# A decoder layer in fp32: the norms behind the output projections, in whole rows of x

## Chip, cores and metric

The kernel runs on one core of one Trainium2 chip. The metric is the device time of one execution in microseconds, the median of several runs.

## The reference

One decoder layer for 2048 tokens of 1024 channels, everything in fp32:

```python
hn = rms_norm(h, mix_pre_g)
proj = hn @ w_in                     # q, k, v and the convolution's input u
attn_out = sliding_window_attention(q, k, v, attn_sinks, rel_bias)   # window 128, 8 heads of 64
conv_out = conformer_conv(u, ...)    # GLU, causal depthwise conv of width 31, LayerNorm, silu, w_conv_pw
mixed = jnp.concatenate([attn_out, conv_out], axis=-1) @ w_out
h = h + rms_norm(mixed, mix_post_g)
hn = rms_norm(h, ffn_pre_g)
ff = (jax.nn.silu(hn @ w_gate) * (hn @ w_up)) @ w_down
h = h + rms_norm(ff, ffn_post_g)
```

`rms_norm(x, g)` is x times the reciprocal root of its mean square, times g. The change concerns the first `h = h + rms_norm(mixed, ...)` and the line behind it, where `hn` is stored without its gain.

## The kernel before

Tokens are worked on in four slices of 512 (w = 0 to 3), each of four tiles of 128 rows. Every large product is made as three fp32r matmuls, from a high and a low part of each operand: ACT copies the high part (`split_w` L123, L127), DVE or POOL subtracts it to get the low part (L129, `lo`). A "product" in the text is one bank of PSUM, 12 or 24 matmuls of 128x512. Names in the profile end in the stage: @A is the input projection (`stage_a`), @B the attention (`stage_b`), @C the convolution (`stage_taps`, `stage_tail`), @W the output projection with its norms (`stage_w` L706, `norm_w` L759), @H the transposes of `hn` into operands of the feed-forward part, @F its gate and up products, @G its down products.

The stages are generators in lanes (`Lane` L1284, `run` L1363): while one stage emits its products, each lane is given credit at a rate, and a stage in a lane emits its next piece when its credit is positive. `yield c` says how much credit a piece costs. A scheduler then orders the instructions of each engine. So W0 stands among the products of A3, W1 ahead of F0, W2 and W3 among those of G0. W_LEAD = 4.0 (L1334) is a piece of that credit, waited at a stage's start.

Tiles come from rotating pools (`BUFS` L53): a new tile of a tag waits until the tile that had its buffer is released. Of 4 KB per partition (one row tile of 1024, or a high and low pair of 512) there are x 4, p 4, mid 4, hl 8, ql 4, chl 5, wx 1; of 2 KB (one half row) gb 2, fa 4, at 2. The tag fa is also A's: ACT puts the block of V into one (L398), from which PE transposes it (L407) and DVE copies it to `vtok` (L410). L418 and a DVE difference put q into `ql`. The tag chl holds operands of W1 to W3. There are four mm banks.

Most loads and stores are issued by SP, in one order: w@A (L126) and raw (L137, L914) weights, mixT (L717), gains `rows` (L697), x (L778, L784), h_scr (L786), keeps (L921), mids and td (L1146, L1150) for G. A DMA that has to wait for its buffer or its data holds up those behind it. ACT's queue issues hn_scr (L797) and mixT (L520).

The norm of one slice goes over its four row tiles `acc[s]`:

1. ACT squares each (L765) with a sum, and `rsqrt` (L144) makes four numbers per partition from them, in 3 small operations on DVE and 12 on POOL (all on DVE for W3).
2. DVE scales `acc[s]` by r and by the gain in two operations of 512 columns (`post_scale` L700, recorded at L94 as are most DVE operations).
3. x is added: one row tile of the four as a whole row in wx, the others as halves in fa or at. For W1 to W3 DVE adds (WV); for W0 POOL adds two of the four row tiles (L779, L785).
4. SP stores the sum to h_scr, ACT squares it (L787).
5. After a second `rsqrt`, ACT scales each row tile in place (L794) and its queue stores hn_scr.

`stage_p1`, `stage_h_plain` and `stage_h_sums` read hn_scr turned, later.

## Time and profile before

| | |
|---|---|
| median of 3 runs | 2044.41 us (2039.39 to 2044.48) |
| the profiled execution | 2052.75 us |
| its span, first to last instruction | 2051.0 us |
| mean granted clock of TensorE | 0.981 |
| busy: PE, DVE, ACT, POOL | 1956.7, 1471.4, 953.2, 367.8 us |

PE is TensorE's matmuls, PEld its weight loads, DVE VectorE, ACT ScalarE, POOL GpSimd, SP the engine that issues most DMAs. A wait is written "engine tile line <- engine tile line": the first waited, for the second, followed by us in total, times and the longest. A row of a timeline has start, duration, engine, line, operation, output <- inputs, shapes, count, and in brackets the idle time before it and what ended it. A group of instructions has its count, busy us, mean ns of one, and the idle time before them with what ended it. The word "issue" in such a bracket means that the profile shows nothing that the engine waited for. The granted clock is TensorE's, as a share of full speed.

### The profile page before, as it was taken

What the parts mean: (1) busy time and instruction counts of PE and PEld (TensorE: products, weight loads), DVE (VectorE), ACT (ScalarE), POOL (GpSimd) and SP (SyncE); (2) the same over time, 40 slices, a digit from 0 to 9 for tenths busy, and PEclk for the clock granted to TensorE, in tenths of its full rate; (3) what the DMA queues carried; (4) which work ended last, traced back from release to release, by engine and by line L of the source; (5) the groups of instructions that cost most, each with busy time, mean ns of one, the idle gap of its engine ahead of it and who ended that gap; (6) DMA issues with size and microseconds to landing.
All of it is one profiled execution on the core that took longest, in us unless ns stands there. A gap on an engine that the chain in (4) does not pass through costs nothing.

```text
span 2051.0 us, 26796 instructions
## 1 busy us (share of the span) xinstructions
PE 1956.7 (95%) x8730; PEld 1556.6 (76%) x8730; DVE 1471.4 (72%) x2583; ACT 953.2 (46%) x1878; POOL 367.8 (18%) x438
## 2 busy tenths in 40 slices
PE   8999998998988899899999989999999999999997
PEld 6777776676756778678878777777878888888886
DVE  4999979967656789788748973678466665545557
ACT  5355354445736634333336454574544434345443
POOL 4012232114011300000000010035323323221003
PEclk9999999999999999999999999999999999999999
DMA  8787655458758875886467787697954443266654
GB/s 301 250 308 237 202 199 184 161 190 267 250 176 280 277 269 196 279 289 202 154 221 240 242 303 232 212 325 242 311 184 153 160 167 113 99 225 225 203 188 148
DMA packets 232028, 454.57 MB, mean 222 GB/s; under 512 B 23208, under 2 KB 48976, under 8 KB 231888
## 3 DMA queue, kind: packets, MB, share of 16 engines
q1 hardware_dynamic: 213648, 426.64, 61.9%
q10 hardware_dynamic: 18240, 26.22, 3.5%
q8 instruction: 69, 1.13, 0.2%
q14 instruction: 71, 0.58, 0.1%
HBM read 331.65 MB, written 121.12 MB: 221 GB/s over the span
## 4 chain that ended last, share of the span: by engine, by line
PE 59%; DMA 16%; DVE 15%; issue 4%; ACT 3%; POOL 2%; SPq 1%; DVEq 0%; ACTq 0%; POOLq 0%
PE mm@F L85 28%; PE mm@G L85 11%; PE mm@A L85 9%; DVE fc@C L94 5%; PE mm@W L85 4%; PE tr@B L85 3%; PE tr@W L85 2%; DVE hl@G L94 2%; DMA mixT<-fc@C 2%; DMA at@W<-mixT 1%; DMA gb@F<-keeps 1%; DVE mid@W L94 1%; DVE w@F L94 1%; DMA td<-fc@G 1%; DVE sm@G L94 1%
## 5 line engine op out<-in xcount | busy, mean ns | idle before, releaser
L94 DVE SCALAR_TENSOR_TENSOR fc@C<-glu@C,colt,fc@C 128x512 f32<-128x512 f32 x480 | 370.6, 790 | 2.6
L85 PE MATMUL mm@F<-hl@H,w@F 128*128 128x512 f32 x1056 | 258.4, 394 | 12.0 <-ACT mm@F L936 10.3
L85 PE MATMUL mm@G<-hl@G,hl@G 128*128 128x512 f32 x924 | 236.0, 395 | 9.8 <-ACT mm@G L1219 3.9
L85 PEld LDWEIGHTS mm@F<-hl@H,w@F 128*128 128x128 f32 x1056 | 199.5, 190 | 57.5 <-ACT mm@F L936 13.5
L85 PE MATMUL mm@A<-hl@A,w@A 128*128 128x512 f32 x840 | 212.5, 400 | 5.1 <-ACT w@A L127 2.4
L85 PEld LDWEIGHTS mm@G<-hl@G,hl@G 128*128 128x128 f32 x924 | 173.4, 190 | 48.4 <-DVE hl@G L94 4.6
L85 PE MATMUL mm@G<-w@G,hl@G 128*128 128x512 f32 x876 | 199.4, 389 | 0.0
L809 ACT ACTIVATE w@F<-chl@F 128x512 fp32r<-128x512 f32 x220 | 134.8, 624 | 129.6 <-PE mm@F L85 122.8
L85 PEld LDWEIGHTS mm@A<-hl@A,w@A 128*128 128x128 f32 x840 | 158.3, 191 | 43.2 <-ACT w@A L127 3.0
L85 PEld LDWEIGHTS mm@G<-w@G,hl@G 128*128 128x128 f32 x876 | 164.4, 188 | 34.2
L94 DVE TENSOR_TENSOR w@F<-chl@F,w@F 128x512 fp32r<-128x512 f32 x198 | 145.0, 734 | 38.6 <-ACT w@F L809 38.3
L85 PE MATMUL mm@F<-ql@H,w@F 128*128 128x512 f32 x528 | 131.5, 397 | 13.6 <-ACT mm@F L1043 5.6
L85 PE MATMUL mm@F<-mid@H,w@F 128*128 128x512 f32 x528 | 132.6, 397 | 0.9 <-DVE fa@F L94 0.3
L85 PE MATMUL mm@F<-p@H,w@F 128*128 128x512 f32 x528 | 130.0, 391 | 0.0
L85 PEld LDWEIGHTS mm@F<-ql@H,w@F 128*128 128x128 f32 x528 | 100.2, 191 | 37.2 <-ACT mm@F L1043 6.6
L85 PE MATMUL mm@F<-x@H,w@F 128*128 128x512 f32 x528 | 127.0, 391 | 0.8 <-ACT fa@F L958 0.8
L85 PEld LDWEIGHTS mm@F<-mid@H,w@F 128*128 128x128 f32 x528 | 100.4, 191 | 23.9 <-ACT mm@F L936 1.1
L85 PEld LDWEIGHTS mm@F<-p@H,w@F 128*128 128x128 f32 x528 | 100.0, 189 | 21.0
L85 PEld LDWEIGHTS mm@F<-x@H,w@F 128*128 128x128 f32 x528 | 98.4, 188 | 22.5 <-ACT fa@F L958 1.3
L127 ACT ACTIVATE w@A<-raw@A 128x512 fp32r<-128x512 f32 x110 | 67.5, 626 | 96.8 <-PE mm@A L85 63.6
L494 POOL TENSOR_SCALAR_AFFINE_SELECT p@B<-p@B 128x512 f32<-128x512 f32 x62 | 51.6, 843 | 278.0 <-ACT p@B L492 276.5
L94 DVE TENSOR_TENSOR w@G<-raw@G,w@G 128x512 fp32r<-128x512 f32 x73 | 52.5, 719 | 67.3 <-ACT w@G L809 66.3
(303 smaller groups left out, 3365.3 us busy)
## 6 DMA issues: line engine op xcount, KB each, us to landing
mids<-fa@F SPq DMA_DIRECT2D x154, 256.0 KB, 2.6
raw@A<-w_in SPq DMA_DIRECT2D x55, 512.0 KB, 4.6
w@A<-lo_in SPq DMA_DIRECT2D x84, 256.0 KB, 3.7
fc@G<-mids SPq DMA_DIRECT2D x77, 256.0 KB, 3.4
fa@G<-mids SPq DMA_DIRECT2D x75, 256.0 KB, 5.0
gb@F<-keeps SPq DMA_DIRECT2D x72, 256.0 KB, 4.2
w@W<-fold SPq DMA_DIRECT2D x32, 512.0 KB, 5.6
chl@F<-w_gate SPq DMA_DIRECT2D x22, 512.0 KB, 3.8
```

What stands on the lines that cost most here:

```text
L85: r = nc.tensor.matmul(*args, **kw)
L94: r = op(*args, **kw)
L127: act(w[:, 0], raw, AF.Copy)
L494: nc.gpsimd.affine_select(out=pg[:, kb].rearrange("p (i q) -> p i q", q=P), in_=pg[:, 1].rearrange("p (i q) -> p i q", q=P), compare_op=AL ...
L809: act(w[:, 0], x, AF.Copy)
```

## The change

- The gain is one whole row tile in chl (before: two halves in gb). The four row tiles of x are whole tiles in chl, asked for as soon as the first `rsqrt` has been emitted (before: halves in fa and at and a whole one in wx, each asked for at its addition).
- The scale is one operation of 1024 columns per row tile (before: two of 512), and so is the addition, always on DVE (before: POOL too for W0; WV is gone).
- The last scale of ACT writes into the x tile rather than in place, and is followed at once by its store to hn_scr; `hns`, which nothing reads, goes.
- The pieces of credit grow: squares 0.5 to 0.75, each scale with its addition 1.5 to 1.25 + 1.25, the last scales 0.1 for all to 1.25 each. W0 gets W_LEAD at its start as well, which only W1 to W3 had.

```diff
@@ -690,20 +690,7 @@
                 vtt(acc[i][:, cs], acc[i][:, cs], o, ALU.add)
             yield 0.65 * len(units)
 
-    def load_gb(row):
-        gb = []
-        for n in range(2):
-            t = f2("gb")
-            nc.sync.dma_start(t, rows[row, n * T : (n + 1) * T].partition_broadcast(P))
-            gb.append(t)
-        return gb
-
-    def post_scale(acc, gb, r):
-        for n in range(2):
-            cs = slice(n * T, (n + 1) * T)
-            stt(acc[:, cs], acc[:, cs], r, gb[n], ALU.mult, ALU.mult)
-
-    def stage_w(w, spill, atag, htags, mtag, bank_of, norm=None, ready=None):
+    def stage_w(w, atag, htags, mtag, bank_of, norm=None, ready=None):
         G = KC // len(htags)
         L = f"W{w}"
         lab[0] = L
@@ -733,8 +720,7 @@
             return ws
 
         nxt = acts(0)
-        if G == 4:
-            yield W_LEAD
+        yield W_LEAD
         for gi in range(KC // G):
             aa = nxt
             for n in range(2):
@@ -750,55 +736,50 @@
                         lab[0] = L
                         nxt = acts(gi + 1)
                     yield c
-        tail = norm_w(w, spill, acc, mtag)
+        tail = norm_w(w, acc)
         if norm:
             norm(tail)
         else:
             yield from tail
 
-    def norm_w(w, spill, acc, mtag):
+    def norm_w(w, acc):
         L = f"W{w}"
         lab[0] = L
-        gb = load_gb(0)
+
+        def whole(src):
+            t = f4("chl")
+            nc.sync.dma_start(t, src)
+            return t
+
+        gb = whole(rows[0].partition_broadcast(P))
         ssq = sm(4)
         for s in range(4):
             act(junk, acc[s], AF.Square, accum_out=ssq[:, s : s + 1])
-            yield 0.5
+            yield 0.75
             lab[0] = L
         r = rsqrt(ssq, 4, D, w < 3)
+        xs = [whole(x[w * T + s * P : w * T + (s + 1) * P]) for s in range(4)]
+        ssq2 = sm(4)
         yield 3
-        lab[0] = L
-        ssq2 = sm(4)
         for s in range(4):
             lab[0] = L
-            post_scale(acc[s], gb, r[:, s : s + 1])
+            stt(acc[s], acc[s], r[:, s : s + 1], gb, ALU.mult, ALU.mult)
+            yield 1.25
+            lab[0] = L
+            vtt(acc[s], xs[s], acc[s], ALU.add)
             r0 = w * T + s * P
-            if s == (2 if mtag == "fa" else 0):
-                xt = f4("wx")
-                nc.sync.dma_start(xt, x[r0 : r0 + P])
-                (vtt if w in WV else ptt)(acc[s], xt, acc[s], ALU.add)
-            else:
-                for n in range(2):
-                    cs = slice(n * T, (n + 1) * T)
-                    xt = f2(mtag if s == 1 or w > 1 else "fa")
-                    nc.sync.dma_start(xt, x[r0 : r0 + P, cs])
-                    (vtt if w in WV or w == 0 and s % 2 else ptt)(acc[s][:, cs], xt, acc[s][:, cs], ALU.add)
             nc.sync.dma_start(h_scr[r0 : r0 + P], acc[s])
             act(junk, acc[s], AF.Square, accum_out=ssq2[:, s : s + 1])
-            yield 1.5
+            yield 1.25
         lab[0] = L
         r2 = rsqrt(ssq2, 4, D, w < 3)
         yield 3
-        lab[0] = L
         for s in range(4):
-            act(acc[s], acc[s], AF.Copy, scale=r2[:, s : s + 1])
-            if spill:
-                r0 = w * T + s * P
-                nc.scalar.dma_start(hn_scr[r0 : r0 + P], acc[s])
-        yield 0.1
-        hns[w] = acc
-
-    hns = {}
+            lab[0] = L
+            act(xs[s], acc[s], AF.Copy, scale=r2[:, s : s + 1])
+            r0 = w * T + s * P
+            nc.scalar.dma_start(hn_scr[r0 : r0 + P], xs[s])
+            yield 1.25
 
     def load_cols(w, k, tag):
         t = f2(tag, (P, 4, P))
@@ -1344,7 +1325,6 @@
     PRES = {0: 20, 2: 16}
     Q0 = 8
     POOL_LO = (3, 6)
-    WV = [1, 2, 3]
     PRE_S0, PRE_S2 = 22, 16
     H1, H2, H3, H4 = 0, 4, 7, 11
     lb = Lane(RB, 0)
@@ -1373,7 +1353,7 @@
 
     lb.add("X", stage_x(), lambda: "x1" in started)
     lu.add("U", stage_fold(), lambda: "A2" in started)
-    lw.add("W0", stage_w(0, True, "x", ["hl"] * 4, "fa", mm), lambda: "A3" in started and "C0" in ld.done and "U" in lu.done)
+    lw.add("W0", stage_w(0, "x", ["hl"] * 4, "fa", mm), lambda: "A3" in started and "C0" in ld.done and "U" in lu.done)
     TGA = [["hl"] * 8, ["mid"] * 4 + ["chl"] * 4, ["hl"] * 8, ["mid"] * 4 + ["hl"] * 4]
     xa = {}
     warm = mm()
@@ -1426,7 +1406,7 @@
     ws, ops = (0, 1), {}
     for n, off in (("B11", 0), ("B21", 4)):
         lh.add(n + ".0", stage_h_plain(ws, ops, n, off))
-    run(stage_w(1, True, "mid", ["hl", "chl"], "at", mm, norm=lambda g: lh.add("N1", g), ready=lambda: stage_pre(ws, ops, mids[0], keeps[0], 0, Q0)))
+    run(stage_w(1, "mid", ["hl", "chl"], "at", mm, norm=lambda g: lh.add("N1", g), ready=lambda: stage_pre(ws, ops, mids[0], keeps[0], 0, Q0)))
     lc.hold = lambda: "S0" not in lh.done
     lh.until("B21.0")
     lh.add("S0", stage_h_sums(ws, ops), lambda: f"P0.{PRE_S0}" in started and "B3" in lb.done)
@@ -1438,9 +1418,9 @@
     lc.rates["T3"] = RC3
     ws, ops = (2, 3), {}
     lw.add("C2", stage_tail(2))
-    lw.add("W2", stage_w(2, True, "mid", ["ql", "chl"], "at", tr))
+    lw.add("W2", stage_w(2, "mid", ["ql", "chl"], "at", tr))
     lw.add("C3", stage_tail(3), lambda: since(lc, "T3", CS))
-    lw.add("W3", stage_w(3, True, "mid", ["ql", "chl"], "at", tr, norm=lambda g: lw.add("N3", g)))
+    lw.add("W3", stage_w(3, "mid", ["ql", "chl"], "at", tr, norm=lambda g: lw.add("N3", g)))
     lw.add("B11.2", stage_h_plain(ws, ops, "B11", 0))
     run(stage_p2((0, 1), mids[0], td))
     lw.until("N3")
```

In the new file the x and gain loads stand at line 751, the squares at 757 and 772, h_scr at 771, the last scale at 779, hn_scr at 781, W's mixT loads and splits at 704 and 706, raw for F at 895.

The scheduler decides what follows from this on each engine. Three places, before and after.

**ACT at W0's norm**. L398 is the copy of V into fa, L418 that of q, L127 a weight's high part, L787 (new: L772) the second squares, L518 and L520 the attention's. Before:

```order
L418 ACTIVATE ql@A_763_4650<-mm@A_761_4618 128x512
L127 ACTIVATE w@A_776_4739<-raw@A_774_4734 128x512
L398 ACTIVATE fa@A_754_4579<-mm@A_753_4554 128x512
L787 ACTIVATE junk,sm@W_742_4508<-x@W_572_3572 128x1024
L518 ACTIVATE at@B_737_4466<-tr@B_736_4461 128x512
L787 ACTIVATE junk,sm@W_742_4508<-x@W_573_3573 128x1024
L520 DMA mixT<-at@B_737_4466 128x4x128
L787 ACTIVATE junk,sm@W_742_4508<-x@W_574_3574 128x1024
L787 ACTIVATE junk,sm@W_742_4508<-x@W_575_3575 128x1024
```

After:

```order
L398 ACTIVATE fa@A_750_4548<-mm@A_749_4523 128x512
L127 ACTIVATE w@A_767_4685<-raw@A_765_4680 128x512
L603 ACTIVATE fc@C_616_3772<-ct@C_615_3767,lnh 128x512
L605 ACTIVATE fc@C_617_3774<-ct@C_615_3767,lnh 128x512
L518 ACTIVATE at@B_731_4439<-tr@B_730_4434 128x512
L127 ACTIVATE w@A_771_4721<-raw@A_770_4719 128x512
L520 DMA mixT<-at@B_731_4439 128x4x128
L772 ACTIVATE junk,sm@W_745_4514<-x@W_572_3572 128x1024
L706 ACTIVATE hl@W_780_4771<-at@W_779_4769 128x512
L418 ACTIVATE ql@A_756_4602<-mm@A_754_4570 128x512
L127 ACTIVATE w@A_772_4724<-raw@A_770_4719 128x512
```

The copy of V has moved ahead of all second squares, and the copy of q and the next split of w@A behind the first of them.

**DVE at the same place**, from the scales to the copy of V into vtok (L410). x@W are the accumulated rows, sm@W the reciprocal roots, fc@C the taps of the convolution. Before, where L410 comes 5 rows behind the last one here:

```order
L94 SCALAR_TENSOR_TENSOR x@W_572_3572<-x@W_572_3572,sm@W_728_4416,gb@W_724_4406 128x512
L94 SCALAR_TENSOR_TENSOR x@W_573_3573<-x@W_573_3573,sm@W_728_4416,gb@W_724_4406 128x512
L94 SCALAR_TENSOR_TENSOR x@W_575_3575<-x@W_575_3575,sm@W_728_4416,gb@W_724_4406 128x512
L94 SCALAR_TENSOR_TENSOR x@W_574_3574<-x@W_574_3574,sm@W_728_4416,gb@W_724_4406 128x512
L94 SCALAR_TENSOR_TENSOR x@W_574_3574<-x@W_574_3574,sm@W_728_4416,gb@W_725_4408 128x512
L94 SCALAR_TENSOR_TENSOR x@W_575_3575<-x@W_575_3575,sm@W_728_4416,gb@W_725_4408 128x512
L94 SCALAR_TENSOR_TENSOR x@W_572_3572<-x@W_572_3572,sm@W_728_4416,gb@W_725_4408 128x512
L94 SCALAR_TENSOR_TENSOR x@W_573_3573<-x@W_573_3573,sm@W_728_4416,gb@W_725_4408 128x512
L94 SCALAR_TENSOR_TENSOR fc@C_705_4284<-glu@C_704_4282,colt,fc@C_705_4284 128x512
L94 TENSOR_TENSOR x@W_573_3573<-fa@W_745_4521,x@W_573_3573 128x512
L94 TENSOR_TENSOR x@W_575_3575<-fa@W_748_4538,x@W_575_3575 128x512
L94 TENSOR_TENSOR x@W_573_3573<-fa@W_746_4524,x@W_573_3573 128x512
```

After:

```order
L94 SCALAR_TENSOR_TENSOR x@W_574_3574<-x@W_574_3574,sm@W_739_4489,chl@W_736_4481 128x1024
L94 SCALAR_TENSOR_TENSOR x@W_573_3573<-x@W_573_3573,sm@W_739_4489,chl@W_736_4481 128x1024
L94 SCALAR_TENSOR_TENSOR x@W_575_3575<-x@W_575_3575,sm@W_739_4489,chl@W_736_4481 128x1024
L94 TENSOR_TENSOR x@W_572_3572<-chl@W_741_4506,x@W_572_3572 128x1024
L94 TENSOR_TENSOR x@W_574_3574<-chl@W_743_4510,x@W_574_3574 128x1024
L94 TENSOR_SCALAR fc@C_700_4256<-glu@C_699_4254,colt 128x512
L94 TENSOR_TENSOR x@W_573_3573<-chl@W_742_4508,x@W_573_3573 128x1024
L94 SCALAR_TENSOR_TENSOR fc@C_617_3774<-fc@C_616_3772,fc@C_617_3774 128x512
L94 TENSOR_TENSOR x@W_575_3575<-chl@W_744_4512,x@W_575_3575 128x1024
L94 SCALAR_TENSOR_TENSOR fc@C_700_4256<-glu@C_699_4254,colt,fc@C_700_4256 128x512
L94 TENSOR_TENSOR hl@W_780_4771<-at@W_779_4769,hl@W_780_4771 128x512
L410 COPY vtok<-mm@A_755_4595 128x512
```

Eight scales of halves and four additions of halves (the fourth comes three rows later, and POOL has three more) have become four scales (the first stands a row ahead of these) and four additions of whole rows, and L410 follows them.

**PE at W0's start**: mm@W are W0's first products, mm@A those of A3, tr@B the attention's. Before:

```order
L85 MATMUL tr@B_542_3408<-kz,ql@A_496_3119 128x256
L85 MATMUL mm@W_583_3596<-w@W_581_3588,hl@W_577_3578 128x512
L85 MATMUL mm@W_584_3604<-w@W_581_3588,hl@W_577_3578 128x512
L85 MATMUL mm@W_585_3612<-w@W_581_3588,hl@W_577_3578 128x512
L85 MATMUL mm@W_586_3620<-w@W_581_3588,hl@W_577_3578 128x512
L85 MATMUL mm@W_585_3612<-w@W_581_3588,hl@W_577_3578 128x512
L85 MATMUL mm@W_584_3604<-w@W_581_3588,hl@W_577_3578 128x512
L85 MATMUL mm@W_586_3620<-w@W_581_3588,hl@W_577_3578 128x512
```

After:

```order
L85 MATMUL tr@B_542_3408<-kz,ql@A_496_3119 128x256
L85 MATMUL mm@W_583_3596<-w@W_581_3588,hl@W_577_3578 128x512
L85 MATMUL mm@W_584_3604<-w@W_581_3588,hl@W_577_3578 128x512 x2
L85 MATMUL mm@A_597_3657<-mid@A_504_3192,w@A_595_3651 128x512 x3
L85 MATMUL mm@W_583_3596<-w@W_581_3588,hl@W_577_3578 128x512
L85 MATMUL mm@A_597_3657<-mid@A_505_3196,w@A_595_3651 128x512 x3
L85 MATMUL mm@A_597_3657<-mid@A_506_3200,w@A_595_3651 128x512 x3
L85 MATMUL mm@A_597_3657<-mid@A_507_3204,w@A_595_3651 128x512 x3
L85 MATMUL mm@A_597_3657<-hl@A_520_3295,w@A_596_3654 128x512 x3
L85 MATMUL mm@A_597_3657<-hl@A_521_3299,w@A_596_3654 128x512 x3
L85 MATMUL mm@A_597_3657<-hl@A_522_3303,w@A_596_3654 128x512 x3
L85 MATMUL mm@A_597_3657<-hl@A_523_3307,w@A_596_3654 128x512 x3
```

A product of A3 stands now behind the first three matmuls of W0, and W0's first banks are filled behind it.

**SP at W1's norm**: raw are the weights of F0, at, fa and (new) chl the rows of x. Before:

```order
L914 DMA raw@F_967_5774<-w_gate 128x512
L914 DMA raw@F_967_5774<-w_up 128x512
L784 DMA at@W_981_5849<-x 128x512
L784 DMA at@W_982_5852<-x 128x512
L914 DMA raw@F_986_5870<-w_gate 128x512
L914 DMA raw@F_986_5870<-w_up 128x512
L914 DMA raw@F_998_5947<-w_gate 128x512
L914 DMA raw@F_998_5947<-w_up 128x512
L784 DMA fa@W_983_5859<-x 128x512
L784 DMA fa@W_984_5862<-x 128x512
L565 DMA y_scr<-fc@C_871_5189 128x512
L540 DMA glu@C_1217_7106<-glu_scr 128x542
```

After:

```order
L895 DMA raw@F_963_5759<-w_gate 128x512
L895 DMA raw@F_963_5759<-w_up 128x512
L751 DMA chl@W_971_5803<-x 128x1024
L751 DMA chl@W_972_5805<-x 128x1024
L751 DMA chl@W_973_5807<-x 128x1024
L895 DMA raw@F_980_5839<-w_gate 128x512
L751 DMA chl@W_974_5809<-x 128x1024
L895 DMA raw@F_980_5839<-w_up 128x512
L895 DMA raw@F_987_5891<-w_gate 128x512
L895 DMA raw@F_987_5891<-w_up 128x512
```

The x rows, before in pairs of halves with two raw tiles between (a pair and the whole row are asked for elsewhere), are now three whole rows one behind the other and the fourth two places on, with raw loads behind them.

## The prediction

> **What bounds the kernel now.** I read the page's first table, then the waits of PE, then the clock and busy time of the 10 us windows in which those waits fall, and last the timelines there.
>
> ```profile
> span 2051.0 us, 26796 instructions
> PE 1956.7 (95%) x8730; PEld 1556.6 (76%) x8730; DVE 1471.4 (72%) x2583; ACT 953.2 (46%) x1878; POOL 367.8 (18%) x438
> ```
>
> PE is busy for 1956.7 of 2051.0 us, so only 94.3 us are idle in the whole span. The change touches no product: PE's instructions stay the same in number and shape. It can gain only what it returns of those 94.3 us, plus what a slow clock costs behind a pause, and lose only what it adds to them. DVE and POOL work saved elsewhere is worth nothing by itself. So the question is which PE waits end on something in the norms. The waits of PE over the whole span, the largest two that concern W0:
>
> ```profile
> PE mm@W L85 <- ACT hl@W L719: 5.1, 1, 5.1
> PE mm@A L407 <- ACT fa@A L398: 4.5, 1, 4.5
> ```
>
> The first is the start of W0's product, the second falls inside W0's norm. The windows around that norm (window, us, then busy time with instruction counts of PE, PEld, DVE, ACT and POOL, then the granted clock, DMA share, GB/s):
>
> ```profile
> 480.00:490.00 10.00, 7.98 (x37) 5.09 (x35) 9.91 (x9) 2.90 (x6) 9.13 (x8) 1.00 0.58 187
> 490.00:500.00 10.00, 5.84 (x16) 4.78 (x17) 9.32 (x13) 5.46 (x10) 1.68 (x2) 0.66 0.59 218
> 500.00:510.00 10.00, 10.00 (x45) 8.26 (x45) 7.55 (x15) 2.90 (x5) 3.88 (x7) 1.00 0.99 319
> ```
>
> PE loses 2.0 us in the first and 4.2 us in the second, where the clock is also 0.66. In the third all is well again. The rows of the timeline in between (start, duration, engine, line, operation, count, and in brackets the idle time before and its releaser):
>
> ```profile
> 480.54 10.02 DVE L94 SCALAR_TENSOR_TENSOR x@W<-x@W,sm@W,gb@W 128x512 f32<-128x512 f32 x8
> 483.05 4.20 POOL L494 TENSOR_SCALAR_AFFINE_SELECT p@B<-p@B 128x512 f32<-128x512 f32 x4
> 487.30 1.94 PE L85 MATMUL tr@B<-p@B,vtok 128*64 128x512 f32 x8 [1.69 <-POOL p@B L494]
> 489.97 1.70 POOL L785 TENSOR_TENSOR x@W<-fa@W,x@W 128x512 f32<-128x512 f32 x1
> 493.51 0.60 ACT L398 ACTIVATE fa@A<-mm@A 128x512 f32<-128x512 f32 x1 [6.75 <-issue]
> 494.16 1.11 PE L407 MATMUL mm@A<-ident,fa@A 128*128 128x128 f32 x4 [4.49 <-ACT fa@A L398]
> 494.93 5.28 PE L85 MATMUL mm@A<-mid@A,w@A 128*128 128x512 f32 x12
> 500.05 2.90 PE L85 MATMUL mm@A<-hl@A,w@A 128*128 128x512 f32 x12
> 497.17 0.69 DVE L410 COPY vtok<-mm@A 128x512 f32<-128x512 f32 x1
>   ACT fa@A L398: 6.7, 1
> ```
>
> The last line is who waited for the POOL additions of line 785. ACT's copy of a V block into an fa buffer (L398) had its data, and yet ACT stood 6.75 us: the four fa buffers were held by halves of x, which the POOL additions read, and POOL came to the second of them only at 489.97, behind eight stretched DVE operations, four selects and a whole-row addition. PE then waited 4.49 us for that copy, and its next 12 matmuls took 5.28 us where the 12 after them took 2.90.
>
> **The change, part by part.**
>
> *Work saved.* The groups of the norms on DVE and POOL (count, busy us, mean ns, idle before):
>
> ```profile
> L94 DVE SCALAR_TENSOR_TENSOR mid@W<-mid@W,sm@W,gb@W 128x512 f32<-128x512 f32 x24 | 16.3, 747 | 8.0 <-POOL sm@W L156 4.9 <-DMA gb@W<-rows 3.1
> L94 DVE SCALAR_TENSOR_TENSOR x@W<-x@W,sm@W,gb@W 128x512 f32<-128x512 f32 x8 | 10.0, 1322 | 0.1
> L94 DVE TENSOR_TENSOR mid@W<-at@W,mid@W 128x512 f32<-128x512 f32 x14 | 9.6, 688 | 4.5 <-DMA at@W<-x 4.5
> L94 DVE TENSOR_TENSOR mid@W<-wx@W,mid@W 128x1024 f32<-128x1024 f32 x3 | 3.7, 1219 | 0.0
> L94 DVE TENSOR_TENSOR mid@W<-fa@W,mid@W 128x512 f32<-128x512 f32 x4 | 2.7, 688 | 0.0
> L94 DVE TENSOR_TENSOR x@W<-fa@W,x@W 128x512 f32<-128x512 f32 x4 | 2.6, 682 | 0.6 <-DMA fa@W<-x 0.6
> L785 POOL TENSOR_TENSOR x@W<-fa@W,x@W 128x512 f32<-128x512 f32 x2 | 3.4, 1712 | 0.9 <-DVE x@W L94 0.9
> L779 POOL TENSOR_TENSOR x@W<-wx@W,x@W 128x1024 f32<-128x1024 f32 x1 | 2.8, 2786 | 0.0
> ```
>
> DVE spends 16.3 + 10.0 + 9.6 + 3.7 + 2.7 + 2.6 = 44.9 us here. The scale of a whole row doesn't occur in this trace. The addition goes from 688 to 1219 ns when its row doubles, 531 ns for 512 columns more, so I put the scale at 747 + 531 = 1278 ns (between 747 and 2 x 747 = 1494). After: 16 x 1.278 + 16 x 1.219 = 40.0 us, 5 us less on DVE and 6.2 us less on POOL. Neither is on the path, PE being the bound, so this term is **0** (if all 5 us of DVE counted, -5).
>
> The Trainium skill, page "VectorE: DVE Perf Modes", gives (N + 151) / 0.96 ns for an operation in fp32 with two tensor operands, which is 1224 ns for 1024 columns; the row of 1219 ns agrees, and the sum doesn't need it.
>
> *W0's norm.* No x row lies in fa any more, so ACT's L398 has a buffer, and in the new order it stands ahead of the second squares (first order piece above). No addition stands on POOL between the selects. That removes the 4.49 us, the 1.69 us behind the selects, and 5.28 - 2.90 = 2.4 us of slow clock that follows the pause: 8.6 us. Instead four scales (5.1 us) and four additions (4.9 us) stand in DVE's queue ahead of the copy of V into vtok (L410) and of the difference of ql, 10 us against 10.02 + 1.88 now; The copy of kz stands just ahead of this burst, and from its bank on PE has by the new order four products of 24 matmuls (4 x 5.8 = 23 us at 2.90 for 12) before it needs a bank that L410 or the difference of ql gives back; the burst with six other operations of 0.7 us between takes about 14, so I see no new wait there. What can bring one is ACT: its second squares stand ahead of the copy of ql (L418) and a split of w@A, and they wait for DVE's first addition, 4 x 1.28 + 1.22 = 6.3 us into the burst. I take **-8**; ends: -9 (everything) and -3 (L398's wait replaced by one of 5 to 6 us behind the squares).
>
> *Start of W0.* Its first wait, on PE and on SP:
>
> ```profile
> 352.41 0.90 SPq L717 DMA_DIRECT2D fa@W<-mixT  x2
> 358.12 7.25 PE L85 MATMUL mm@W<-w@W,hl@W 128*128 128x512 f32 x20 [5.08 <-ACT hl@W L719]
> 369.37 2.29 PE L85 MATMUL mm@W<-w@W,hl@W 128*128 128x512 f32 x6 [1.96 <-ACT x@W L688]
> ```
>
> W_LEAD, which W0 didn't have, puts A3's products beside the start of W0. By the new order A3 matmuls stand among the first of W0, so the second pause (1.96 us, a bank) gets cover; the first one depends on the mixT load, which stands now behind a store of lo_out instead of two w@A loads. Such stores wait for POOL's split of the weight, before W0's start up to this long:
>
> ```profile
> SPq L131 <- POOL w@W L129: 9.5, 4, 4.5
> ```
>
> Since that weight is also loaded earlier, I take about the same moment as now, and **-3**; ends +4 (the load stands behind such a wait) and -7 (5.08 + 1.96).
>
> *W1's norm.* The x rows share the chl buffers with W1's operand, and on SP their loads stand amid raw loads for F0 (last order piece). Now:
>
> ```profile
> 612.43 9.34 SPq L784 DMA_DIRECT2D at@W<-x  x2
> SPq L784 <- DMA mixT<-at@B: 8.6, 1, 8.6
> 622.13 19.20 PE L85 MATMUL mm@F<-x@H,w@F 128*128 128x512 f32 x84
> 633.71 3.94 SPq L784 DMA_DIRECT2D fa@W<-x  x2
> 637.71 0.90 SPq L921 DMA_DIRECT2D gb@F<-keeps  x2
> 650.00:660.00 10.00, 8.10 (x36) 6.32 (x36) 0.31 (x2) 5.14 (x8) 2.37 (x12) 1.00 1.04 403
> ```
>
> SP already stands for 8.6 us of the 9.34 on the second at buffer, and comes free at 621.8. After the change it waits instead for chl buffers that W1's last matmuls release at about 622: the same moment. Then four rows of 512 KB, 2.1 MB, are asked for at once, with two raw tiles (0.5 MB each) behind or among them. At 319 GB/s, as in the window from 500 to 510, 2.1 MB is 6.6 us. PE has seven products of 12 matmuls (84 in 19.20 us, 2.74 each) there, of which three, 8.2 us, were split ahead: covered. The keeps loads, which now wait until the scales let go of gb (637.71), go earlier by some microseconds, and PE's pauses at 650 to 660 come behind those. I take **-1**; ends -4 and +4 (one batch of x not covered).
>
> *W2 and W3.* These run beside G0's products.
>
> ```profile
> SPq L786 <- DVE mid@W L94: 9.8, 2, 9.2
> 1188.98 0.32 SPq L786 DMA_DIRECT2D h_scr<-mid@W  x1
> 1190.82 18.44 PE L85 MATMUL mm@G<-hl@G,hl@G 128*128 128x512 f32 x80 [1.72 <-DVE hl@G L94]
> 1211.37 3.91 PE L85 MATMUL mm@G<-hl@G,hl@G 128*128 128x512 f32 x16 [2.11 <-DVE p@G L1179]
> ```
>
> SP stands 9.2 us at the h_scr store until DVE has finished a row, with fa@G loads behind it, and PE loses 1.72 and 2.11 us just there. The change keeps the store with its wait; the loads of x in halves between the stores go, and W3's last product comes 17 G0 matmuls later. Gain and loss look alike: **-1**, ends -6 (both pauses and one more of that size) and +6.
>
> *More yields.* A norm now takes 24 units of its lane where it took 14.1, so its instructions are spread over about 1.7 times as many products. The consumers (H's transposes) have slack by the order, so 0.
>
> **Sum:** 0 - 8 - 3 - 1 - 1 = -13; I round it to **-12**, since each term supposes that nothing takes the place of its pause. The profiled execution was 2052.75 us (span 2051.0), so it would be about 2040.8; against the median of 2044.41, on which the forecast is made, 2032.4.
>
> **The rivals.**
>
> 1. *The x rows hold up SP (slower).* SP issues in order; an x load that waits for a chl buffer holds up every load behind it. For it: the 8.6 us and 9.2 us that SP stands now at lines of the norm. Against: 2.1 MB is covered by 8.2 us of products. It decides where the wait plus 6.6 us of transfer exceeds 8.2 us, so from a buffer that comes 1.6 us late. At W1, W2 and W3 it would cost PE up to one batch, 3 x 6.6 = 20 us; with the 11 us of W0 gained it ends at +9, **2053**.
>
> 2. *Another wait takes the place of W0's (same).* ACT's squares, behind the DVE burst, hold up L418 and the split of w@A, so that PE pauses about as long and drops to 0.66 again. Of W0's 8.6 us only 3 are gained, with -1 at its start: **2040**.
>
> 3. *Whole-row operations stretch POOL (half the gain).* The same scale took 1322 ns beside POOL's additions and 747 ns without, so DVE and POOL do hinder each other here. POOL still has the selects and the rsqrt in this stretch: with 4 selects, each held up by one scale of 1.28 us, PE's wait for p@B grows by up to 5 us and eats half of the 11: -6, **2038**. The Trainium skill states such a rule ("SBUF — State Buffer", section "Who interferes with whom"): a DVE instruction that takes two SBUF inputs and a GpSimd instruction lock each other out, for the whole instruction. By that rule a row of 1024 holds the port longer at a time than two of 512 do; the trace agrees with it only by the pair 1322 and 747.
>
> That the change doesn't do what it says isn't open: no POOL addition and no fa or at load of x is left in the new order.
>
> **How the numbers follow.** Forecast (2026 to 2036): 0.45. Rival 3 (2036 to 2041): 0.15. Rival 2 (about 2040): 0.15. Rival 1 (2046 to 2058): 0.17. More gain than forecast, by the far ends of W1 to W3 (2016 to 2026): 0.08. A measurement here can tell about 0.3% from no change, that is 2038.3 and 2050.5. Faster: 0.45 + 0.08 + two thirds of rival 3 + a fifth of rival 2 = 0.66. Slower: the upper four fifths of rival 1, 0.14. Same: 0.20. The far ends of the terms add to -31 and +11: I leave out the lowest 0.05 and the top 0.07 of rival 1, so 2018 to 2054.
>
> **What would show it.** W0's norm: the wait of PE at the transposes of V (4.49 us) is gone, the window at 490 to 500 is over 9 us busy at clock 1.0, and the copy at L398 waits for no buffer. If a wait for ql or w@A, and a low clock, stand there instead, rival 2 holds. W0's start: the waits of 5.1 and 2.0 us shrink. W1: SP's wait at the x loads ends near 622 and PE's pauses between 600 and 720 don't exceed today's. If they do, with releasers among raw, w@F or the fa and mb loads of G0, rival 1 holds. The scale of a row: 1278 ns; over 1500 beside POOL work speaks for rival 3. The forecast is wrong if PE's busy time itself grows, or if pauses elsewhere, where lanes meet anew, sum to more than 10 us.

## The result, and the profile after

| | before | after |
|---|---|---|
| median of 5 runs each | 2044.48 us (2039.39 to 2051.95) | 2029.11 us (2024.85 to 2033.98) |
| profiled execution, span | 2051.0 us | 2025.9 us |
| PE busy | 1956.7 us | 1943.8 us |
| PE idle (span less busy) | 94.3 us | 82.1 us |

The ratio is 0.9922, 95% interval 0.9893 to 0.9951: 15 us less, with 10 to 22 us in the interval. The two profiled executions differ by 25 us; part of that is chance, as the repeated kernels below show (two profiles of before: 2051.0 and 2046.9; of after: 2025.9 and 2029.7).

The page of the changed kernel, first table:

```profile
span 2025.9 us, 26731 instructions
PE 1943.8 (96%) x8730; PEld 1550.0 (77%) x8730; DVE 1457.7 (72%) x2558; ACT 954.0 (47%) x1878; POOL 365.7 (18%) x435
```

PE has the same 8730 matmuls and is idle for 12 us less. Its busy time fell by 13 us with the same work, which is what the clock accounts for: the mean granted clock went from 0.981 to 0.987, and 1956.7 x 0.981 / 0.987 = 1944.8. Three 10 us windows around W0's norm, whose first scale now starts at 470.84 instead of 480.54 (columns as in the prediction):

```profile
470.00:480.00 10.00, 10.00 (x49) 7.05 (x48) 9.16 (x9) 6.31 (x12) 0.60 (x3) 1.00 0.87 277
480.00:490.00 10.00, 10.00 (x46) 8.29 (x45) 8.75 (x17) 6.81 (x13) 1.39 (x2) 1.00 0.99 309
490.00:500.00 10.00, 10.00 (x49) 7.53 (x48) 7.36 (x11) 4.24 (x6) 5.64 (x11) 1.00 0.86 319
```

PE is full at clock 1.00 in all three, where the first two of before's had 7.98 and 5.84 us, the second at clock 0.66. The timeline there: ACT's copy of V, DVE's burst, PE's transposes of V (L407), DVE's copy into vtok and its difference of q, PE's first scores with q (tr@B<-kz,ql@A), ACT's last scales:

```profile
469.62 0.60 ACT L398 ACTIVATE fa@A<-mm@A 128x512 f32<-128x512 f32 x1 [0.89 <-PE mm@A L85]
470.84 4.87 DVE L94 SCALAR_TENSOR_TENSOR x@W<-x@W,sm@W,chl@W 128x1024 f32<-128x1024 f32 x4 [1.68 <-POOL sm@W L156]
475.63 2.35 DVE L94 TENSOR_TENSOR x@W<-chl@W,x@W 128x1024 f32<-128x1024 f32 x2
477.43 0.60 PE L407 MATMUL mm@A<-ident,fa@A 128*128 128x128 f32 x4
482.50 0.68 DVE L410 COPY vtok<-mm@A 128x512 f32<-128x512 f32 x1
483.10 0.68 DVE L94 SCALAR_TENSOR_TENSOR ql@A<-mm@A,ql@A 128x512 fp32r<-128x512 f32 x1
494.32 0.97 PE L85 MATMUL tr@B<-kz,ql@A 64*128 64x256 f32 x11
496.50 2.19 ACT L779 ACTIVATE chl@W<-x@W,sm@W 128x1024 f32<-128x1024 f32 x2 [4.29 <-POOL sm@W L156]
```

V is copied at 469.62, as soon as PE has it and 1.2 us before the first scale; before, it was 13.0 us after it (493.51 against 480.54). L410 comes 11.7 us after the first scale and no PE wait ends on it. PE's order has changed too: between the transposes of V and the first scores there are now 72 matmuls, three products of q. Before, the first four scores stood ahead of the transposes (494.16):

```profile
489.17 0.50 PE L85 MATMUL tr@B<-kz,ql@A 64*128 64x256 f32 x4
```

The groups of the norms on DVE, and what SP and PE wait for at W0's start and W1's norm:

```profile
L94 DVE SCALAR_TENSOR_TENSOR mid@W<-mid@W,sm@W,chl@W 128x1024 f32<-128x1024 f32 x12 | 14.6, 1279 | 3.0 <-POOL sm@W L156 3.0
L94 DVE TENSOR_TENSOR mid@W<-chl@W,mid@W 128x1024 f32<-128x1024 f32 x12 | 14.3, 1216 | 0.0
L94 DVE SCALAR_TENSOR_TENSOR x@W<-x@W,sm@W,chl@W 128x1024 f32<-128x1024 f32 x4 | 4.9, 1278 | 1.7 <-POOL sm@W L156 1.7
L94 DVE TENSOR_TENSOR x@W<-chl@W,x@W 128x1024 f32<-128x1024 f32 x4 | 4.8, 1216 | 0.0
```

```profile
SPq L751 <- PE mm@W L85: 8.0, 3, 5.3
```

```profile
PE mm@W L85 <- ACT hl@W L706: 3.7, 2, 3.2
PE mm@F L85 <- ACT mm@F L917: 4.2, 4, 1.6
```

SP's row is from 590 to 640 us and the last row from 600 to 720; before, the last wait was 10.3 us. W0's start still has a wait of 3.2 us where it had 5.1 (3.8 in the second profile of before).

### The profile page after: what moved, and what is told of

Its sections match the earlier page's. It is cut to its first block, busy times and chain, and to the rows that moved or that the text cites. A ratio compares the mean times of both kernels' runs of the same rounds, so it can differ in the third digit from the quotient of the medians.

```text
span 2025.9 us, 26731 instructions
## 1 busy us (share of the span) xinstructions
PE 1943.8 (96%) x8730; PEld 1550.0 (77%) x8730; DVE 1457.7 (72%) x2558; ACT 954.0 (47%) x1878; POOL 365.7 (18%) x435
## 4 chain that ended last, share of the span: by engine, by line
PE 41%; DMA 11%; DVE 9%; issue 3%; POOL 2%; ACT 2%; SPq 0%; ACTq 0%; DVEq 0%; POOLq 0%
PE mm@F L85 24%; PE mm@G L85 13%; PE tr@W L85 3%; DMA gb@F<-keeps 2%; DVE w@F L94 1%; DVE chl@F L94 1%; DMA td<-fc@G 1%; DMA chl@F<-w_gate 1%; DVE fa@F L94 1%; DVE fc@C L94 1%; DMA wx@G<-h_scr 1%; DVE sm@G L94 1%; DMA chl@F<-w_up 1%; DVE hl@G L94 1%; DVE x@G L94 1%
## 5 line engine op out<-in xcount | busy, mean ns | idle before, releaser
L85 PE MATMUL mm@F<-hl@H,w@F 128*128 128x512 f32 x1056 | 253.4, 390 | 5.5 <-ACT mm@F L917 4.2
L85 PE MATMUL mm@G<-hl@G,hl@G 128*128 128x512 f32 x924 | 230.3, 394 | 2.9 <-ACT hl@G L790 2.5
L127 ACT ACTIVATE w@A<-raw@A 128x512 fp32r<-128x512 f32 x110 | 67.3, 626 | 87.6 <-PE mm@A L85 58.6
```

The source lines that it names most:

```text
L85: r = nc.tensor.matmul(*args, **kw)
L127: act(w[:, 0], raw, AF.Copy)
```

## The experiments

Two theories stood against each other at first. **Buffers and POOL**, the prediction's: the copy of V was late because halves of x, waiting for POOL's additions, held its buffers. **Shift**, the rival: W_LEAD moves W0's norm behind the V block, whatever the buffers.

All runs in one table. The ratio is against runs of before on the same chip, in brackets its interval. "V" is the start of V's copy (L398) less that of W0's first scale. The other columns are stretches of each kernel's PE timeline: *start* from three quarters of all mm@A matmuls to a quarter of all mm@W; *norm* from there to the last mm@W (W0's norm, W1); *F0* from there to the first mm@G; *G0* from there to the last tr@W (W2, W3). The bounds are taken at rows of the timeline; taken at single matmuls a stretch differs by up to 0.9 us.

| run | ratio | V | start | norm | F0 | G0 |
|---|---|---|---|---|---|---|
| before, first profile | | +13.0 | 80.5 | 206.7 | 433.5 | 251.3 |
| before_again | 0.9996 [0.9982, 1.0010] | +13.0 | 80.6 | 207.0 | 435.4 | 249.7 |
| dve_adds | 1.0014 [1.0003, 1.0025] | +11.6 | 80.2 | 209.7 | 435.0 | 249.8 |
| chl_x | 1.0005 [0.9990, 1.0020] | +1.5 | 79.6 | 204.8 | 438.0 | 249.8 |
| w123_new | 1.0018 [1.0003, 1.0034] | +13.0 | 78.7 | 208.5 | 432.4 | 250.4 |
| no_lead | 0.9959 [0.9946, 0.9971] | +1.2 | 79.9 | 194.1 | 434.6 | 248.5 |
| lead_only | 0.9949 [0.9936, 0.9963] | +0.1 | 75.8 | 197.9 | 435.0 | 251.3 |
| w0_new | 0.9950 [0.9934, 0.9965] | -1.5 | 77.5 | 195.8 | 437.1 | 250.2 |
| pool_adds | 0.9957 [0.9939, 0.9974] | -0.9 | 75.3 | 200.6 | 429.5 | 248.0 |
| old_yields | 0.9938 [0.9922, 0.9953] | -1.3 | 78.2 | 195.4 | 434.2 | 248.8 |
| lead_dve | 0.9931 [0.9912, 0.9950] | +0.8 | 73.7 | 194.4 | 435.0 | 248.2 |
| half_ops | 0.9902 [0.9876, 0.9927] | -0.6 | 76.1 | 193.9 | 433.4 | 254.0 |
| after, first profile | 0.9922 [0.9893, 0.9951] | -1.2 | 74.9 | 195.7 | 430.6 | 248.5 |
| after_again | 0.9915 [0.9899, 0.9932] | -1.7 | 76.2 | 193.4 | 429.9 | 248.6 |

**lead_only**: W_LEAD alone.

```diff
-        if G == 4:
-            yield W_LEAD
+        yield W_LEAD
```

> Before, with W_LEAD at W0's start as the only edit (x rows in fa, at and wx, POOL additions, operations of 512 as before). If the freed fa buffers and the missing POOL additions are what ended the stall in W0's norm, PE still waits some 4 us for the copy of V (L398's line) or for a successor of it, and only W0's start gains, about 3 to 6 us: 2039 to 2041 against 2044.5. If the shift by W_LEAD is what did it (the copy of V now stands in ACT's order ahead of the second squares), the wait for the copy of V is gone here too and the time is within 3 us of the changed kernel's 2029.

2038.54 us against 2049.72, so 11 us gained: between the buffers' theory (3.5 to 5.5 us) and the shift's (12.5 or more). The profile is what the shift's gave: V's copy waits for PE only, though x still lies in fa.

```profile
472.96 0.60 ACT L398 ACTIVATE fa@A<-mm@A 128x512 f32<-128x512 f32 x1 [1.71 <-PE mm@A L85]
484.70 1.06 ACT L786 ACTIVATE junk<-x@W 128x1024 bf16<-128x1024 f32 x1 [5.44 <-DVE x@W L94]
500.69 2.20 ACT L793 ACTIVATE x@W<-x@W,sm@W 128x1024 f32<-128x1024 f32 x2 [3.55 <-POOL sm@W L156]
505.53 4.83 PE L85 MATMUL mm@W<-w@W,hl@W 128*128 128x512 f32 x20 [2.42 <-ACT hl@W L719]
```

With V's copy out of the way, a new wait stands some 30 us later. ACT works in order; its last scales (L793) wait for the second rsqrt, and a split of W1's operand (hl@W) stands behind them. PE waits 2.42 us for that.

**no_lead**: all of the change except W_LEAD for W0.

```diff
-        yield W_LEAD
+        if G == 4:
+            yield W_LEAD
```

> The changed kernel without W_LEAD for W0. By the buffers: the copy of V waits for no buffer, PE has no wait over 2 us in W0's norm, and what is lost is W0's start, 3 to 6 us: 2032 to 2035. By the shift: PE's stall of 4 us and a granted clock below 0.9 come back in W0's norm, 2040 or more.

2041.33 us. No PE wait over 1 us is left between 400 and 515, the *norm* stretch is the shortest but two, and *start* is 79.9, as in kernels without the lead. The mechanism is the buffers' one; by time it loses more than the 3 to 6 us expected, about 9 of 17 (0.9959 against 0.9915). By the stretches about 4 of these lie in *start* and 4 in F0, none in the norm.

**dve_adds**: before, with no additions of x on POOL.

```diff
-    WV = [1, 2, 3]
+    WV = [0, 1, 2, 3]
```

> Before, with all of W0's additions of x on DVE rather than two row tiles on POOL; x still in fa. If POOL's additions made the copy of V late, ACT's wait ahead of it falls from 6.75 us to under 3 and PE's from 4.5 to under 1.5, gain 5 to 8 us: 2037 to 2040. If the fa buffers make it late whoever adds, the copy still waits over 4 us, and the time stays within 3 us of 2044.5.

2052.15 us, a little slower than before: the time is what the theory of the fa buffers gave, the place of the wait isn't. POOL was not the single cause. PE's wait of 4.5 us has only moved to the next block, q:

```profile
481.80 6.88 DVE L94 SCALAR_TENSOR_TENSOR x@W<-x@W,sm@W,gb@W 128x512 f32<-128x512 f32 x8
486.05 0.60 ACT L418 ACTIVATE ql@A<-mm@A 128x512 fp32r<-128x512 f32 x1 [2.08 <-PE mm@A L85]
493.47 0.68 DVE L94 SCALAR_TENSOR_TENSOR ql@A<-mm@A,ql@A 128x512 fp32r<-128x512 f32 x1
494.20 0.58 PE L85 MATMUL tr@B<-kz,ql@A 64*128 64x256 f32 x2 [5.89 <-DVE ql@A L94]
```

ACT has the high part of q at 486.65, and DVE comes to the difference at 493.47, behind eight scales and five additions. This is the prediction's second rival, met in a variant: a burst of the norm on an engine in order, ahead of something that PE needs at once.

**chl_x**: before, with W0's x in chl.

```diff
         r = rsqrt(ssq, 4, D, w < 3)
+        xs = []
+        for s in range(4 if w == 0 else 0):
+            xs.append(f4("chl"))
+            nc.sync.dma_start(xs[s], x[s * P : (s + 1) * P])
...
-            if s == (2 if mtag == "fa" else 0):
+            if w == 0:
+                (vtt if s % 2 else ptt)(acc[s], xs[s], acc[s], ALU.add)
+            elif s == 0:
```

> Before, with W0's four x rows as whole tiles in chl, asked for right after the first rsqrt; the scales still of 512, POOL still adds two rows (whole ones, 2.8 us each), no W_LEAD. By the buffers: the copy of V waits for no buffer, PE's 4.5 us and the slow clock behind go, the wait behind the selects may stay (1.7 us) since POOL still adds: gain 6 to 7, 2037 to 2039. By POOL: two additions of 2.8 us hold up selects and second squares, PE's wait stays over 3 us, within 3 us of 2044.5.

2050.26 us, no change, as the theory of POOL had it in time but not in its reason. V's copy is free (480.31, right behind the first scale at 478.85) and PE's 4.5 us at it are gone. Other waits take their place at W1's start (this profile is of the slowest of the kernel's 12 executions, 2057.09 us, so I read from it where PE waits rather than how long):

```profile
485.65 0.60 ACT L418 ACTIVATE ql@A<-mm@A 128x512 fp32r<-128x512 f32 x1 [2.09 <-PE mm@A L85]
490.13 1.06 ACT L793 ACTIVATE junk<-x@W 128x1024 bf16<-128x1024 f32 x1 [3.36 <-POOL x@W L781]
503.82 0.63 ACT L719 ACTIVATE hl@W<-at@W 128x512 fp32r<-128x512 f32 x1 [6.71 <-DMA at@W<-mixT]
```

```profile
SPq L792 <- DVE x@W L94: 5.4, 2, 5.1
SPq L717 <- DMA mixT<-at@B: 4.3, 1, 4.3
```

```profile
PE mm@W L85 <- ACT chl@W L719: 3.8, 3, 2.7
PE mm@W L85 <- ACT hl@W L719: 2.5, 2, 1.9
PE mm@W L85 <- DMA w@W<-lo_out: 1.9, 1, 1.9
```

(SP's rows are from 490 to 530 us, PE's from 500 to 630.) SP stood 5.1 us at a store of h_scr and 4.3 us at a load of mixT; W1's operand (at@W) then arrives late. Freeing the buffers is not enough.

**w0_new** and **w123_new**: the changed norm for W0 alone (with W_LEAD), and for W1 to W3 alone. `norm_old` and `norm_new` are `norm_w` of before and after.

```diff
-        tail = norm_w(w, spill, acc, mtag)
+        tail = norm_old(w, spill, acc, mtag) if w else norm_new(w, acc)    # w0_new
+        tail = norm_new(w, acc) if w else norm_old(w, spill, acc, mtag)    # w123_new
```

> Before, with the changed norm and W_LEAD for W0 alone; W1 to W3 keep the old norm. If the gain is W0's, nearly all of it is here: 2029 to 2033. If W1 to W3 carry a third or more of it, 2034 to 2039.

> Before, with the changed norm for W1, W2 and W3 alone; W0 is as before, stall and all. If the gain is W0's: 2041 to 2046. If W1 to W3 carry a third or more: 2035 to 2040. If the x rows' loads hold up SP there (the slower rival) and W0's gain covers it: over 2047.

2037.57 and 2050.24 us. W0 carries about 10 us; W1 to W3 by themselves carry nothing, rather a loss of 0.2%. w0_new lies in the second branch of its expectation, w123_new by its time in the third, that of the slower rival; but F0, behind the x loads, is no longer there than in before (432.4 against 433.5 and 435.4), so the profile doesn't show that rival. And the two don't add up: 0.9950 x 1.0018 = 0.9968, and the whole is 0.9915. By the stretches, w0_new lacks 6 to 7 us that the changed kernel has in F0 (437.1 against 430.6 and 429.9) and has most of W0's gain; w123_new shows 432.4 there, in between, and 208.5 in *norm*.

**half_ops**: after, with operations of 512.

```diff
-            stt(acc[s], acc[s], r[:, s : s + 1], gb, ALU.mult, ALU.mult)
+            for n in range(2):
+                cs = slice(n * T, (n + 1) * T)
+                stt(acc[s][:, cs], acc[s][:, cs], r[:, s : s + 1], gb[:, cs], ALU.mult, ALU.mult)
...
-            vtt(acc[s], xs[s], acc[s], ALU.add)
+            for n in range(2):
+                cs = slice(n * T, (n + 1) * T)
+                vtt(acc[s][:, cs], xs[s][:, cs], acc[s][:, cs], ALU.add)
```

> The changed kernel with two scales and two additions of 512 columns for each whole one; buffers, engines, loads and yields as changed. DVE gets 16 x (2 x 747 - 1278) + 16 x (2 x 688 - 1217) ns = 6 us more. If DVE's work is off the path: within 3 us of 2029. If whole-row operations are what helped: 2035 or more. If they hinder POOL by holding a shared port longer: below 2026.

2028.11 us, ratio 0.9902: as good as the whole rows (0.9915 and 0.9922). No gain or loss by the width of the operations can be seen.

**pool_adds**: after, with POOL adding to two of W0's row tiles.

```diff
-            vtt(acc[s], xs[s], acc[s], ALU.add)
+            (vtt if w or s % 2 else ptt)(acc[s], xs[s], acc[s], ALU.add)
```

> The changed kernel with POOL adding x to W0's row tiles 0 and 2 (whole rows, 2.8 us each). If POOL's additions were part of the stall: PE waits again for selects or squares in W0's norm, 2032 to 2036. If the buffers alone did it: within 3 us of 2029, no PE wait over 2 us there.

2038.61 us, 0.9957: half of the gain is lost. The rows show two effects of POOL's additions:

```profile
474.40 9.13 DVE L94 SCALAR_TENSOR_TENSOR x@W<-x@W,sm@W,chl@W 128x1024 f32<-128x1024 f32 x4 [1.68 <-POOL sm@W L156]
475.76 6.68 POOL L769 TENSOR_TENSOR x@W<-chl@W,x@W 128x1024 f32<-128x1024 f32 x2 [1.40 <-DVE x@W L94]
499.82 2.19 ACT L779 ACTIVATE chl@W<-x@W,sm@W 128x1024 f32<-128x1024 f32 x2 [6.58 <-POOL sm@W L156]
505.66 0.58 PE L85 MATMUL tr@B<-kz,ql@A 64*128 64x256 f32 x2 [5.47 <-ACT ql@A L418]
```

Four scales that took 4.87 us take 9.13 beside POOL's two additions, and the last of the four additions ends 12.5 us after the first scale's start, where it was 10.5. And ACT's order is another: the copy of the third q (L418, at 505.03) now stands behind the last scales, where ACT waits 6.58 us, and PE waits 5.47 us for that copy. In the changed kernel the copy of the third q stands ahead of them:

```profile
488.99 0.60 ACT L418 ACTIVATE ql@A<-mm@A 128x512 fp32r<-128x512 f32 x1 [1.59 <-PE mm@A L85]
```

The last scales themselves come no later than there, counted from V's copy (26.3 us against 26.9).

**lead_dve**: before with the edits of lead_only and dve_adds, and nothing else: two lines.

> Before, with two one-line edits: W_LEAD at W0's start, and all of W0's additions on DVE; x still in fa, at and wx, operations of 512, old norm for W1 to W3. If the lead and the missing POOL additions are all that W0 needs, buffers and whole rows being free: at least 15 us under before, as half_ops (ratio 0.990 to 0.993). If the freed buffers matter beside them: a new wait for a buffer or for ql in W0's norm and no more than lead_only (ratio 0.995). If W1 to W3 carry the rest: about w0_new, 0.995, with no wait in W0's norm.

2031.60 us against 2047.05, 0.9931. x lies in fa, at and wx, in halves; nothing of W1 to W3 is changed.

```profile
471.07 5.39 DVE L94 SCALAR_TENSOR_TENSOR x@W<-x@W,sm@W,gb@W 128x512 f32<-128x512 f32 x8 [0.66 <-POOL sm@W L156]
471.89 0.60 ACT L398 ACTIVATE fa@A<-mm@A 128x512 f32<-128x512 f32 x1 [1.71 <-PE mm@A L85]
482.24 0.68 DVE L94 SCALAR_TENSOR_TENSOR ql@A<-mm@A,ql@A 128x512 fp32r<-128x512 f32 x1
```

The trace shows no wait of PE between 400 and 515 us. The lead alone gives 0.5%, the additions on DVE alone nothing, both together 0.7% and most of the gain. The intervals of lead_only and lead_dve overlap; what POOL's additions cost is measured more clearly by pool_adds against after_again (0.9957 and 0.9915, intervals apart). And w0_new, which has both edits and the rest of the change at W0, came to 0.9950, also with overlapping intervals: W0 alone carries 10 to 14 of the 17 us. So neither theory holds by itself: the shift clears the V block, without POOL's additions no other wait takes its place in the norm, and the freed buffers are not needed for this part. What the whole change has beyond lead_dve (0.9915 against 0.9931) is within the intervals.

**before_again** and **after_again**: unchanged.

> The kernel before, unchanged, for a second profile and as a measure of noise. Ratio 1.000 within 0.002. If the first profile of before is typical, the stage from the last of W1's products to the last of G's takes 1416 us again, and PE's stall at the copy of V is there again (4 us or more); if that stage is 3 us or more shorter, the 4 to 6 us by which kernels with the new norm in W1 to W3 seemed to gain there were that one profile's.

> The changed kernel, unchanged, on the same chip as the variants. If single edits and the whole add up: ratio 0.992 again, PE without a wait over 1 us in W0's norm. If chip or day made the difference between it (0.992) and w0_new (0.995): 0.994 to 0.996.

2046.74 us (0.9996) and 2029.07 us (0.9915). Before's two profiles agree on every stretch of the table within 2 us, V's copy and its 4.5 us included; what differs is the stretch ahead of W0, which no edit touches (335.1 and 331.3 us up to three quarters of mm@A; after: 331.3 and 336.1). So the 25 us between the first two profiles hold 3 to 4 us of chance ahead of the change.

**old_yields**: after, with the old pieces of credit, W_LEAD kept.

```diff
-            yield 0.75
+            yield 0.5
...
-            yield 1.25
-            lab[0] = L
             vtt(acc[s], xs[s], acc[s], ALU.add)
...
-            yield 1.25
+            yield 1.5
...
-            yield 1.25
+        yield 0.1
```

> The changed kernel with the old pieces of credit (squares 0.5, scale and addition together 1.5, the last scales 0.1 for all), W_LEAD kept. If spreading the norm over more products helps, as the forecast gave it nothing: 4 us or more over the changed kernel, with new waits of PE where the pieces bunch. If not: within 3 us of it.

2034.17 us, 0.9938: about 5 us over the changed kernel, though the intervals just overlap. By the stretches it would lie in *start* (78.2 against 74.9 and 76.2) and F0 (434.2 against 430.6 and 429.9), but its profiled execution (2039.02 us) is the slowest of its six, and half_ops, which loses nothing, has 433.4 in F0. I found no single wait that carries it.

## Why the prediction was right, and where it was not

- **The bound.** PE is the bound, and engines beside it count for nothing by themselves: shown. DVE's norms went from 44.9 to 38.6 us (14.6 + 14.3 + 4.9 + 4.8; forecast 40.0), and giving 3.5 us of this back in half_ops (42.1 us) costs no time. The forecast's 40.0 is 32 operations times their mean, which comes to 39.9 here; 44.9 and 38.6 are busy time, in which operations that overlap count once, so the forecast saving of 5 us set one measure against the other. The scale of a whole row was put at 1278 ns from two other rows, and is 1278.
- **W0's norm, -8.** All three pieces of the stall (4.5, 1.7 and 2.4 us) went, as forecast. By the stretch *norm* it is -12.3 (means 206.9 and 194.6), more than the 8.6 us that the stall costs in PE and clock; where the rest comes from was not traced. The reason given has two parts, "No x row lies in fa any more, so L398 has a buffer", and no addition on POOL. Together, and with the rest of the change, they are enough without W_LEAD (no_lead, 194.1). The freed buffers alone are not (chl_x has no x in fa, and no gain), and they are not needed (lead_dve has x in fa, and 194.4).

  The wait of V's copy was also read wrongly. POOL's second addition ended at 491.67, but the copy started at 493.51, just behind the second of three additions by DVE, which ended at 493.43 (before):

```profile
492.15 1.88 DVE L94 TENSOR_TENSOR x@W<-fa@W,x@W 128x512 f32<-128x512 f32 x3
```

  So it was DVE's additions, 1.8 us later than POOL's, that let the copy go.

  What the kernels without a stall at V or the first q share is PE's order: V's transposes and three products of q ahead of the first scores. before, before_again, w123_new and dve_adds have the first scores ahead of the transposes. V's copy on ACT comes ahead of the burst or just behind its start, but DVE's difference of q still comes behind the burst, 12.3 us after the first scale (483.10); it has time, since the scores come only at 494.32. W_LEAD brings this order, and so do the freed buffers (no_lead, chl_x). Beside it the additions had to leave POOL, or another wait came in (lead_only, pool_adds).
- **W0's start, -3.** The mean of *start* is 76.0 in the eight profiles with the lead and 79.9 in the six without: -4. The size was right, the waits only in part: the second pause, which was to get cover, is still 1.6 us in two (1.1 in after_again) where it was 2.0, and the first, put at about the same moment as now, went to 3.2 and 3.1 us from 5.1 and 3.8. And W_LEAD was counted only here. Without freed buffers it gives most of the norm's gain (lead_only, 197.9); with them it adds nothing to the norm (no_lead, 194.1). The order piece on ACT showed V ahead of the squares, and I put that down to the buffers.
- **W1, -1.** SP waits 8.0 us for chl buffers, as it had for at (8.6), and PE's pauses behind it became a little smaller: the wait shown above went from 10.3 to 4.2 us, while one of 2.5 us for gb@F is new in one of the two profiles. That wait divides the runs cleanly: 3.9 to 5.7 us in the seven profiles with the new norm for W1, 8.3 to 10.3 in the seven without, w123_new (4.7) and lead_dve (8.8) included. The stretch F0 has a mean of 432.1 in the first seven and 435.6 in the others: -3.5, inside the ends of -4 and +4, though the two groups overlap. What of it is left at the end is not shown: from the last mm@W to the last mm@G lead_dve takes 1411.9 us with the old norm, no_lead 1416.5 with the new one.
- **W2 and W3, -1.** G0's means are 249.5 and 250.0 by the same division. A term that could as well be 0.
- **More yields, 0.** Mis-sized: old_yields puts about 5 us on them, at the edge of what its runs tell apart.
- **Sum.** Forecast -12, measured -15.4 (-10 to -22), and -17 in the later runs (0.9915 of 2047). The terms that seem too small (W0's norm, W1, the yields) have one sign. The stretches together give about -20, more than the medians, since the profiled executions of before (2052.75 and 2048.64 us) are slower than its medians; so each term is known to a few us only. That the sum falls in the forecast's range is partly luck: its largest term rests on a wait that was read wrongly, as told above, and no run tells how the terms that were too small share the rest.
- **The rivals.** The first (SP held up) didn't occur: SP waits for chl as it waited for at, and F0 behind it got no longer, in w123_new either. The second is real, and three variants fell to it: DVE's burst ahead of ql (5.9 us in dve_adds), ACT's last scales ahead of q (5.5 us in pool_adds) and ahead of W1's operand (2.4 us in lead_only). In the changed kernel the largest wait of this kind is 0.5 us, for W1's operand. The third isn't seen: half_ops shows nothing by width, and its condition didn't come about, since POOL's four selects ran from 466.64 to 469.80, ahead of the first scale (470.84). The exclusion between DVE and POOL on which it rested is there, with the additions: 9.13 us against 4.87. That agrees with the Trainium skill, "SBUF — State Buffer", section "Who interferes with whom": a DVE instruction with two SBUF inputs and a GpSimd instruction that reads SBUF keep each other out. The change profits from it, as it takes the additions from POOL, and the price that I gave the rule stood at the wrong pair: at the selects and whole rows, instead of the additions that go.

What stays open: why w0_new and w123_new don't add up to the whole, although w123_new has the shorter waits in F0 too, and which wait the yields take away. No run separated the early loads of x from the rest, and none tells why W_LEAD or free buffers make the scheduler put the scores behind the products of q.

## What to carry to other kernels

When PE waits for a small copy that had its data, find out what stands ahead of it in its engine's order, and ask first whether the whole burst can be moved by a few products; clearing only the cause that the profile names may hand the wait to the next block. A side engine that shares the work of a burst can make the burst longer rather than shorter: two additions on POOL cost four DVE scales 4.3 us here. And of two edits that each give nothing or half, the pair may give nearly all: test them together before adding machinery.

## What was not expected of the hardware

- The small POOL operations of the rsqrt (4 elements per partition) come in two lengths. In the changed kernel, first rsqrt and second:

```profile
465.10 0.20 POOL L153 TENSOR_TENSOR sm@W<-sm@W 128x4 f32<-128x4 f32 x1 [8.54 <-DVE sm@W L94]
488.53 0.69 POOL L153 TENSOR_TENSOR sm@W<-sm@W 128x4 f32<-128x4 f32 x1 [17.73 <-DVE sm@W L94]
```

  The same operation takes 0.20 or 0.69 us, 0.5 more, and most of the second chain's twelve have the long form, on a stretch where DVE was busy for 8.75 and 7.36 of each 10 us. The kept profiles show what goes with it. Of the 1008 such operations in the 14 profiles, 294 start while a DVE operation with two inputs from SBUF is running, and 291 of these take over 0.3 us; of the other 714, 2 do.
- Two executions of one program differ by 3 to 5 us in a stretch of 335 us that no edit touches. A difference of a few us between two single profiles is read stretch by stretch, or not at all.
